# Down projection of a hybrid decoder block: weight sums on VectorE, half-row weight loads, the residual added late

## The chip, the cores and the metric

The kernel runs on one core of one Trainium2 chip. The metric is the device time of one execution in microseconds (us), as the median of repeated runs. Engines are named as the profile names them: PE (TensorE matmul) with PEld (its weight loads), DVE (VectorE), ACT (ScalarE), POOL (GpSimd) and SP (SyncE, which here only issues DMAs).

## The reference

A decoder block on 1024 tokens of width 1024, all in float32: a token mixer (forgetting attention beside HGRN2), a cross-attention over 256 memory rows, and a gated ConvFFN. Each is wrapped in `LN(ALPHA * x + f(x))`. Only the last part matters here:

```
u = x @ w_up                      # 1024 x 1024 by 1024 x 5632
u = causal_conv3(u) + conv_b      # per channel
a, g = split(u)
ff = (silu(g) * a) @ w_down       # 1024 x 2816 by 2816 x 1024
x = layer_norm(ALPHA * x + ff, ln3_g, ln3_b)
```

## The kernel before

float32 products are made from two fp32r parts. `split` (L181 on) makes them: ACT casts a tile to its high part (L183), and DVE or POOL subtracts that from the tile to get the low part (L185). Each product then takes three matmuls: high by high, high by low, low by high.

**Up stage** (L1080 and around). 22 blocks `f` of 128 hidden channels. `begin(f)` and `end(f)` run seven Strassen-Winograd products per block, the convolution and the gate follow on ACT and DVE, and the hidden tile `za` (128 channels x 1024 tokens) is written to DRAM as `hid_dram[f]` (L1125). POOL splits the weights of this stage (L1047) and forms some of their sums (L1024).

**Down stage** (L1162 on). The product with `w_down` is again Strassen-Winograd: halves over tokens, over the 22 hidden blocks (11 and 11, `HC`) and over output columns. `plan` lists seven **passes** q = 0..6. Each names a factor A of hidden tiles (A11, S3, S2, A22, S1, A12, S4), a factor B of weight rows (B11, T3, T2, T4, T1, B21, B22), and which group of four PSUM banks it accumulates in. A pass has 11 **steps** i, and a step is four token tiles by three matmuls, 12 matmuls 128x128 by 128x512 (L1239). Pass 6 runs four steps, and then the last seven (`DROWS`) for one token tile after the other, so that the closing LayerNorm can follow row by row.

For each step `load_step(q, i)` prepares two operands, called `dop`:

- `rows_of` loads hidden tiles into `raw`, a ring of three buffers. For S3, S2, S1 and S4 DVE adds or subtracts two of them (L1204). S3 and S2 are also stored to DRAM (L1206), since later passes build on them.
- `factor` fetches weight rows with `row(half, i)` (L1167 to L1172, one load of 512 KB into a 4 KB-a-partition slot `wr`) and forms T3, T2, T4, T1 in place, on POOL (L1179, L1181, L1183, L1185). It asks for both halves in every pass but the first. The slots of half 0 are given up after T1 (pass 4); from pass 5 on `factor` calls `row(0, i)` again, which loads those 11 rows a second time.
- both are split, with the subtraction on DVE.

Steps are prepared up to seven ahead (`DAHEAD`) if at least four of the 47 slots are free. Slots are handed out first in, first out.

The output rows `ys` (eight tiles of 128 x 1024) are loaded from `x2_dram` before passes 0 and 1 (L1246). After a pass, DVE moves the four banks out: the first part of a half row as `y = ALPHA*y + ps` (`scaled`, L1262), later ones as `y = y + ps` (`added`, L1263, L1285). After pass 4 rows 4 to 7 are finished and get their LayerNorm; after pass 6 rows 0 to 3. `layer_norm` takes statistics and a scale on DVE (L782, L787), a power on POOL (L785), a scale on ACT (L793) and adds the bias on POOL (L794). The store follows on SP, and the slot is given back.

**What sets the order.** The program is written in the order above, but a scheduler in the build moves instructions: it places each on its engine when its own estimate says that the inputs are ready. On the chip each engine then runs its list strictly in order, so an instruction that waits holds up all behind it on its engine. This holds for SP too, whose list is made of DMA issues.

Of the kernel before, what the change touches and what calls it, by code (L numbers as in the profile page):

```python
# [15 lines left out]
P = 128  # L16
# [86 lines left out]
def hybrid_block(ctx: ExitStack, tc: tile.TileContext, x, mem, w_in, b_fox_f, lb_logits, norm_g, w_out,  # L103
# [180 lines left out]
    def hs(half):  # L284
        return slice(half * 512, (half + 1) * 512)
# [819 lines left out]
    def end(f):  # L1105
        ya, yg, pa = live.pop(f)
        pc, pd = bank("t"), bank("t")
        product(f, "S3", "T3", pc, True)
        nc.scalar.copy(yg[:, hs(1)], pc)  # L1109
        product(f, "S1", "T1", pd, True)  # L1110
        nc.vector.tensor_tensor(yg[:, hs(1)], yg[:, hs(1)], pd, ALU.add)
        product(f, "S2", "T2", pa, False)
        u = small.tile([P, 512], F32, tag="vT", name="u", bufs=1)
        nc.scalar.copy(u, pa)
        nc.vector.tensor_tensor(yg[:, hs(1)], yg[:, hs(1)], u, ALU.add)
        product(f, "A22", "T4", pc, False)
# [48 lines left out]
    wrow, loaded = {}, {}  # L1165

    def row(half, i):  # L1167
        if (half, i) not in wrow:
            wrow[half, i] = get([P, 2, 512], name="wr")
            r = (half * HC + i) * P  # L1170
            nc.sync.dma_start(wrow[half, i].rearrange("p n c -> p (n c)"), w_down[r:r + P, :])
        return wrow[half, i]  # L1172

    def factor(name, i):

        lo, hi = row(0, i), row(1, i) if name != "B11" else None
        tt = nc.gpsimd.tensor_tensor
        if name == "T3":
            tt(lo[:, 1], hi[:, 1], lo[:, 1], ALU.subtract)  # L1179
        if name == "T2":  # L1180
            tt(lo[:, 1], lo[:, 1], lo[:, 0], ALU.add)  # L1181
        if name == "T4":
            tt(lo[:, 0], hi[:, 0], lo[:, 1], ALU.subtract)  # L1183
        if name == "T1":
            tt(lo[:, 1], hi[:, 1], lo[:, 1], ALU.subtract)  # L1185
        if name in ("B21", "B22"):
            return hi[:, int(name == "B22")]
        return lo[:, int(name not in ("B11", "T4"))]

    def rows_of(name, i):  # L1190

        h0, h1, s3, s2 = hid_dram[i], hid_dram[HC + i], sum_dram[0][i], sum_dram[1][i]
        a11, a12, a22 = h0[:, hs(0)], h1[:, hs(0)], h1[:, hs(1)]
        if name in ("A11", "A12", "A22"):
            raw = rawp.tile([P, 512], F32, tag="raw", name="raw")
            nc.sync.dma_start(raw, {"A11": a11, "A12": a12, "A22": a22}[name])
            return raw
        raw = rawp.tile([P, 2, 512], F32, tag="raw", name="raw")
        if name == "S3":
            nc.sync.dma_start(raw.rearrange("p j s -> p (j s)"), h0)  # L1200
        else:
            for j, src in enumerate({"S2": (a22, s3), "S1": (s2, a11), "S4": (a12, s2)}[name]):
                nc.sync.dma_start(raw[:, j], src)
        nc.vector.tensor_tensor(raw[:, 0], raw[:, 0], raw[:, 1], ALU.add if name == "S1" else ALU.subtract)  # L1204
        if name in ("S3", "S2"):
            nc.sync.dma_start(s3 if name == "S3" else s2, raw[:, 0])  # L1206
# [24 lines left out]
    for q, (a, b, g, first) in enumerate(plan):  # L1231
        if first:
            groups[g] = [bank(tag) for tag in (("S", "S", "S", "t"), ("t", "t", "pj", "pj"))[g]]

        def part(t, i, lo=0, hi=512):
            x, w = loaded[q, i]
            ss = slice(t * P, (t + 1) * P)
            for n, (xp, wp) in enumerate(((0, 0), (0, 1), (1, 0))):
                nc.tensor.matmul(groups[g][t][:, lo:hi], x[:, xp, ss], w[:, wp, lo:hi],  # L1239
                                 start=first and i == 0 and n == 0, stop=i == HC - 1 and n == 2,  # L1240
                                 skip_group_check=not first)

        if q < 2:
            for t in range(4 * q, 4 * q + 4):
                ys[t] = get([P, D], name="y")
                nc.sync.dma_start(ys[t], x2_dram[t * P:(t + 1) * P, :])  # L1246
        if q == 4:
            gb = load_gb(ln3_g, ln3_b)
        last = q == len(plan) - 1
        inner = HC - DROWS if last else HC  # L1250
        for i in range(inner):
            fill(q * HC + i + DAHEAD)
            for t in range(4):
                part(t, i)
# [65 lines left out]
```

## Time and profile before

| | us |
|---|---|
| median of 3 runs | 1637.95 (1633.11 to 1639.56) |
| the profiled execution: its own time | 1632.78 |
| its span (first to last instruction) | 1630.9 |
| DVE busy in the span | 1093.8 (67%) |
| POOL busy in the span | 702.9 (43%) |
| down stage, first to last matmul | 1359.87 to 1621.01 |

Times in the trace count from the span's start. In a list of groups, a line is: source line, engine, operation, tiles out<-in, shape, count, then busy time, mean duration in ns, and idle time of that engine just before, with what ended it. In a timeline, a line is start, length, engine, line, operation, and in brackets the idle time before it with its releaser. In a table of windows, each engine has its busy time and its number of instructions; the last three columns are the granted TensorE clock (1 is the full 2.4 GHz, 0.5 is 1.2 GHz), the share of time that the DMA engines were busy, and GB/s.

### The profile page before, as it was taken

What the parts mean: (1) busy time and instruction counts of PE and PEld (TensorE: products, weight loads), DVE (VectorE), ACT (ScalarE), POOL (GpSimd) and SP (SyncE); (2) the same over time, 40 slices, a digit from 0 to 9 for tenths busy, and PEclk for the clock granted to TensorE, in tenths of its full rate; (3) what the DMA queues carried; (4) which work ended last, traced back from release to release, by engine and by line L of the source; (5) the groups of instructions that cost most, each with busy time, mean ns of one, the idle gap of its engine ahead of it and who ended that gap; (6) DMA issues with size and microseconds to landing.
All of it is one profiled execution on the core that took longest, in us unless ns stands there. A gap on an engine that the chain in (4) does not pass through costs nothing.

```text
span 1630.9 us, 21374 instructions
## 1 busy us (share of the span) xinstructions
PE 1552.6 (95%) x7949; PEld 1305.6 (80%) x7949; DVE 1093.8 (67%) x1698; ACT 734.9 (45%) x1301; POOL 702.9 (43%) x540
## 2 busy tenths in 40 slices
PE   8999998999998999999999999999999998789977
PEld 6788887888887988888978877888888887668856
DVE  3856967567667756623567568777666679787777
ACT  4726554256657742133442154454544445234341
POOL 5302122233436731112003658787677774850053
PEclk9999999999999999999999999999999999899989
DMA  5301112222132673202472212232222247765763
GB/s 182 78 1 27 53 52 61 60 75 78 46 111 66 181 238 110 103 27 65 138 239 78 91 39 78 95 100 78 78 78 91 79 162 255 259 221 185 259 219 109
DMA packets 164455, 185.31 MB, mean 114 GB/s; under 512 B 7584, under 2 KB 122344, under 8 KB 164352
## 3 DMA queue, kind: packets, MB, share of 16 engines
q1 hardware_dynamic: 160864, 172.26, 33.5%
q10 hardware_dynamic: 3168, 11.54, 1.9%
q8 instruction: 62, 1.02, 0.3%
q14 instruction: 41, 0.34, 0.1%
q0 software_dynamic: 320, 0.16, 0.1%
HBM read 141.42 MB, written 38.31 MB: 110 GB/s over the span
## 4 chain that ended last, share of the span: by engine, by line
PE 64%; DVE 14%; DMA 10%; POOL 4%; ACT 4%; issue 3%; SPq 0%; DVEq 0%; POOLq 0%; ACTq 0%
PE ps_pj L174 19%; PE ps_S L174 17%; PE ps_t L1080 11%; PE ps_S L1080 6%; PE ps_t L174 4%; DVE dop L185 3%; PE ps_pj L1080 3%; DMA raw<-hid 3%; DMA raw<-sumS 2%; DVE raw L1204 1%; DMA raw<-in_w_out_dram 1%; PE ps_t L650 1%; POOL y L794 1%; POOL wop L1047 1%; PE ps_t L213 1%
## 5 line engine op out<-in xcount | busy, mean ns | idle before, releaser
L174 PE MATMUL ps_pj<-xT,wh 128*128 128x512 f32 x976 | 313.0, 396 | 0.9 <-DVE KL L593 0.9
L185 POOL TENSOR_TENSOR wl<-raw,wh 128x1024 fp32r<-128x1024 f32 x48 | 120.6, 2512 | 223.3 <-ACT wh L183 208.5
L174 PEld LDWEIGHTS ps_pj<-xT,wh 128*128 128x128 f32 x976 | 180.0, 188 | 35.2 <-DVE KL L593 1.4
L1080 PE MATMUL ps_t<-T,wop 128*128 128x512 f32 x792 | 191.9, 393 | 2.8 <-ACT yg L1109 2.1
L174 PE MATMUL ps_pj<-xT,wl 128*128 128x512 f32 x488 | 192.6, 395 | 0.0
L1080 PEld LDWEIGHTS ps_t<-T,wop 128*128 128x128 f32 x792 | 149.2, 189 | 35.2 <-ACT yg L1109 2.5
L1047 POOL TENSOR_TENSOR wop<-raw,wop 128x512 fp32r<-128x512 f32 x66 | 110.7, 1689 | 89.3 <-ACT wop L1046 89.2
L1047 POOL TENSOR_TENSOR wop<-sw,wop 128x512 fp32r<-128x512 f32 x88 | 135.3, 1560 | 21.8 <-ACT wop L1046 21.8
L784 POOL TENSOR_SCALAR mv<-mv 128x1 f32<-128x1 f32 x24 | 24.3, 1016 | 256.0 <-DVE mv L783 256.0
L1239 PE MATMUL ps_S<-dop,dop 128*128 128x512 f32 x396 | 104.5, 406 | 13.2 <-DVE dop L185 12.6
L1239 PE MATMUL ps_t<-dop,dop 128*128 128x512 f32 (+1 forms) x351 | 94.9, 392 | 19.7 <-ACT dop L183 13.1
L174 PEld LDWEIGHTS ps_pj<-xT,wl 128*128 128x128 f32 x488 | 91.8, 188 | 17.6
L1239 PEld LDWEIGHTS ps_S<-dop,dop 128*128 128x128 f32 x396 | 76.2, 195 | 34.3 <-DVE dop L185 17.0
L174 PE MATMUL ps_S<-wh,mh 128*128 128x512 f32 x256 | 100.1, 391 | 0.6 <-ACT mh L183 0.6
L174 PE MATMUL ps_S<-wh,ml 128*128 128x512 f32 x256 | 100.2, 392 | 0.0
L174 PE MATMUL ps_S<-wl,mh 128*128 128x512 f32 x256 | 99.9, 390 | 0.0
L183 ACT CAST dop<-raw 128x512 fp32r<-128x512 f32 x77 | 47.5, 620 | 105.6 <-DVE raw L1204 73.1
L1239 PEld LDWEIGHTS ps_t<-dop,dop 128*128 128x128 f32 x351 | 65.0, 195 | 36.4 <-ACT dop L183 15.2
L183 ACT CAST wh<-raw 128x1024 fp32r<-128x1024 f32 x64 | 67.2, 1050 | 59.8 <-issue 23.3
L1046 ACT CAST wop<-sw 128x512 fp32r<-128x512 f32 x88 | 54.6, 622 | 86.2 <-POOL sw L1024 57.9
L185 DVE TENSOR_TENSOR dop<-raw,dop 128x512 fp32r<-128x512 f32 x77 | 65.4, 855 | 17.4 <-ACT dop L183 16.5
L185 DVE TENSOR_TENSOR dop<-wr,dop 128x512 fp32r<-128x512 f32 x77 | 67.2, 886 | 10.9 <-ACT dop L183 10.8
(299 smaller groups left out, 3608.9 us busy)
## 6 DMA issues: line engine op xcount, KB each, us to landing
raw<-in_ffn_w_up_dram SPq DMA_DIRECT2D x44, 512.0 KB, 3.9
raw<-hid SPq DMA_DIRECT2D x66, 256.0 KB, 3.6
wr<-in_ffn_w_down_dram SPq DMA_DIRECT2D x33, 512.0 KB, 5.6
raw<-in_w_in_dram SPq DMA_DIRECT2D x24, 512.0 KB, 4.0
hid<-z SPq DMA_DIRECT2D x22, 512.0 KB, 2.6
raw<-sumS SPq DMA_DIRECT2D x33, 256.0 KB, 4.2
raw<-in_xa_wkv_dram SPq DMA_DIRECT2D x16, 512.0 KB, 4.5
x_dram<-y ACTq DMA_DIRECT2D x16, 512.0 KB, 2.6
```

The costliest lines, as they stand in the source:

```text
L174: nc.tensor.matmul(o, l, r, start=start, stop=stop)
L183: nc.scalar.copy(h, src)
L185: eng.tensor_tensor(l, src, h.bitcast(F32), ALU.subtract)
L213: nc.tensor.transpose(ps[:, k * P:(k + 1) * P], nat[:, kk * P:(kk + 1) * P], ident)
L650: nc.tensor.transpose(tp[:, b * P:(b + 1) * P], pr[1 - b % 2][:, c * P:(c + 1) * P], ident)
L784: nc.gpsimd.tensor_scalar(mv[:, 2:3], mv[:, 1:2], LN_EPS, None, ALU.add)
L794: nc.gpsimd.tensor_tensor(yp, yp, b[:, lo:hi], ALU.add)
L1046: nc.scalar.copy(w[:, 0], src)
L1047: nc.gpsimd.tensor_tensor(w[:, 1], src, w[:, 0].bitcast(F32), ALU.subtract)
L1080: nc.tensor.matmul(ps, w[:, part, ws], r, start=first and k == 0 and i == 0, stop=k == 3 and i == 2, skip_group_check=not first)
L1204: nc.vector.tensor_tensor(raw[:, 0], raw[:, 0], raw[:, 1], ALU.add if name == "S1" else ALU.subtract)
L1239: nc.tensor.matmul(groups[g][t][:, lo:hi], x[:, xp, ss], w[:, wp, lo:hi], start=first and i == 0 and n == 0, stop=i == HC - 1 and n == 2, ...
```

## The change

Six edits, all but the first in the down stage:

- **S3 made in the up stage.** For the first 11 blocks `f`, DVE subtracts the two token halves of `za` right after the gate, and SP stores the result to `sum_dram`. Pass 1 then loads 256 KB a step in place of 512 KB, with no DVE operation and no store.
- **Sums of weights on DVE.** T3, T2, T4 and T1 move from POOL to DVE, 44 instructions of 128x512.
- **Weight rows in halves.** `row(half, n, i)` loads 256 KB, one column half, when it is first asked for. Passes 5 and 6 no longer ask for half 0, so its 11 reloads are gone.
- **First parts by ACT.** The 16 `scaled` moves become plain copies on ACT (`taken`).
- **Residual late.** `x2` rows are loaded in passes 4 and 5 (steps 4 to 7) into a slot, and DVE adds them with `y = ALPHA*x + y` (L1261, 128x1024, eight times).
- **Output rows keep their slots** to the end, and `ln3`'s gains are loaded at step 3 of pass 4.

```diff
         nc.sync.dma_start(hid_dram[f], za)
+        if f < HC:
+            s3 = get([P, 512], name="s3")
+            nc.vector.tensor_tensor(s3, za[:, hs(0)], za[:, hs(1)], ALU.subtract)
+            nc.sync.dma_start(sum_dram[0][f], s3)
+            put(s3)
...
-    def row(half, i):
+    def row(half, n, i):
         if (half, i) not in wrow:
             wrow[half, i] = get([P, 2, 512], name="wr")
+        t = wrow[half, i][:, n]
+        if (half, n, i) not in here:
+            here.add((half, n, i))
             r = (half * HC + i) * P
-            nc.sync.dma_start(wrow[half, i].rearrange("p n c -> p (n c)"), w_down[r:r + P, :])
-        return wrow[half, i]
+            nc.sync.dma_start(t, w_down[r:r + P, hs(n)])
+        return t
...
-        lo, hi = row(0, i), row(1, i) if name != "B11" else None
-        tt = nc.gpsimd.tensor_tensor
+        tt = nc.vector.tensor_tensor
+        if name in ("B11", "B21", "B22"):
+            return row(int(name[1]) - 1, int(name[2]) - 1, i)
+        t = row(0, int(name != "T4"), i)
         if name == "T3":
-            tt(lo[:, 1], hi[:, 1], lo[:, 1], ALU.subtract)
+            tt(t, row(1, 1, i), t, ALU.subtract)
...
-                nc.sync.dma_start(ys[t], x2_dram[t * P:(t + 1) * P, :])
...
+            if (q in (4, 5)) and 4 <= i < 8:
+                t = i - 4 if q == 5 else i
+                x = get([P, D], name="x2")
+                nc.sync.dma_start(x, x2_dram[t * P:(t + 1) * P, :])
+                nc.vector.scalar_tensor_tensor(ys[t], x, ALPHA, ys[t], ALU.mult, ALU.add)
+                put(x)
...
-            scaled = lambda y, cs: nc.vector.scalar_tensor_tensor(y[:, cs], y[:, cs], ALPHA, ps, ALU.mult, ALU.add)
+            taken = lambda y, cs: nc.scalar.copy(y[:, cs], ps)
...
-                put(y)
```

The first place is DVE's list in pass 0. In the kernel before, `dop_11902` and `dop_11924` are the weight operands of steps 6 and 7, `z_11817` is the last hidden tile of the up stage:

```order
L1123 TENSOR_TENSOR z_11817<-z_11817,z_11799 128x1024
L185 TENSOR_TENSOR dop_12090<-wr_11867,dop_12090 128x512
L185 TENSOR_TENSOR dop_11902<-wr_11897,dop_11902 128x512
L185 TENSOR_TENSOR dop_11965<-raw,dop_11965 128x512
L185 TENSOR_TENSOR dop_11987<-raw,dop_11987 128x512
L185 TENSOR_TENSOR dop_12115<-wr_11877,dop_12115 128x512
L185 TENSOR_TENSOR dop_11921<-raw,dop_11921 128x512
L185 TENSOR_TENSOR dop_11924<-wr_11919,dop_11924 128x512
```

In the changed kernel, steps 6 and 7 have the weight operands `dop_11931` and `dop_11953`; the last hidden tile stands two rows above these:

```order
L1190 TENSOR_TENSOR wr_11916<-wr_12157,wr_11916 128x512
L185 TENSOR_TENSOR dop_11931<-wr_11926,dop_11931 128x512
L1194 TENSOR_TENSOR wr_11876<-wr_12061,wr_11876 128x512
L1192 TENSOR_TENSOR wr_11886<-wr_11886 128x512
L185 TENSOR_TENSOR dop_12139<-wr_11906,dop_12139 128x512
L1192 TENSOR_TENSOR wr_11896<-wr_11896 128x512
L185 TENSOR_TENSOR dop_12016<-raw,dop_12016 128x512
L185 TENSOR_TENSOR dop_12163<-wr_11916,dop_12163 128x512
L1194 TENSOR_TENSOR wr_11886<-wr_12085,wr_11886 128x512
L185 TENSOR_TENSOR dop_11950<-raw,dop_11950 128x512
L1192 TENSOR_TENSOR wr_11906<-wr_11906 128x512
L185 TENSOR_TENSOR dop_11953<-wr_11948,dop_11953 128x512
```

The sums L1190 (T3, for pass 1), L1192 (T2, for pass 2) and L1194 (T4, for pass 3) now stand between the operands that pass 0 waits for.

The second place is SP's list around the start of pass 6. In the kernel before, rows 4 to 7 are stored (`out_dram`) after the loads of step 1, and a reload of half 0 (`wr_13324`) stands among them:

```order
L1203 DMA raw<-hid_7591 128x512
L1203 DMA raw<-sumS_1_7613 128x512
L1290 DMA out_dram<-y_12163 128x1024
L1290 DMA out_dram<-y_12165 128x1024
L1203 DMA raw<-hid_7592 128x512
L1203 DMA raw<-sumS_2_7614 128x512
L1203 DMA raw<-hid_7593 128x512
L1290 DMA out_dram<-y_12167 128x1024
L1171 DMA wr_13324<-in_ffn_w_down_dram 128x1024
L1203 DMA raw<-sumS_3_7615 128x512
L1290 DMA out_dram<-y_12169 128x1024
```

In the changed kernel:

```order
L1207 DMA raw<-sumS_4_7616 128x512
L1207 DMA raw<-hid_7595 128x512
L1207 DMA raw<-sumS_5_7617 128x512
L1300 DMA out_dram<-y_12186 128x1024
L1300 DMA out_dram<-y_12187 128x1024
L1207 DMA raw<-hid_7596 128x512
L1300 DMA out_dram<-y_12188 128x1024
L1207 DMA raw<-sumS_6_7618 128x512
L1300 DMA out_dram<-y_12189 128x1024
L1207 DMA raw<-hid_7597 128x512
```

The stores now come after the loads of step 5, and no reload is left.

## Rows read from the trace of the kernel before

**Rows 1.** Line L1239 (the down matmuls): what its engine waited for, us, times.

```profile
  DVE dop L185: 43.0, 26
  ACT dop L183: 30.0, 14
```

**Rows 2.** Windows: an up stretch, passes 0 to 4, then 5 and 6 together.

```profile
core 0: us, PE busy (x) PEld busy (x) DVE busy (x) ACT busy (x) POOL busy (x), PEclk, DMA share, GB/s
960.00:1160.00 200.00, 196.95 (x871) 161.81 (x870) 143.38 (x131) 99.31 (x143) 152.53 (x94) 0.99 0.25 79
...
1359.90:1409.50 49.60, 39.88 (x150) 31.53 (x149) 43.11 (x38) 17.85 (x28) 33.72 (x20) 0.86 0.76 273
1409.50:1448.90 39.40, 32.13 (x130) 24.48 (x128) 33.96 (x30) 11.46 (x19) 30.75 (x20) 0.96 0.64 219
1448.90:1482.90 34.00, 31.63 (x132) 24.44 (x133) 25.83 (x35) 11.89 (x21) 7.49 (x5) 1.00 0.71 235
1482.90:1513.20 30.30, 30.21 (x133) 24.70 (x132) 24.95 (x41) 14.79 (x26) 0.00 (x0) 1.00 0.50 156
1513.20:1544.10 30.90, 30.27 (x134) 24.72 (x133) 22.24 (x36) 11.38 (x20) 0.00 (x0) 1.00 0.80 266
1544.10:1621.00 76.90, 64.10 (x286) 51.63 (x284) 57.48 (x86) 27.50 (x44) 30.33 (x20) 0.91 0.51 174
```

**Rows 3.** PE's timeline at five places of the down stage.

```profile
1396.05 2.93 PE L1239 MATMUL ps_S<-dop,dop 128*128 128x512 f32 x6 [3.98 <-DVE dop L185]
...
1484.29 1.52 PE L1239 MATMUL ps_pj<-dop,dop 128*128 128x512 f32 x6
1485.65 1.52 PE L1239 MATMUL ps_t<-dop,dop 128*128 128x512 f32 x6
...
1564.47 1.52 PE L1239 MATMUL ps_pj<-dop,dop 128*128 128x512 f32 x6
1576.31 0.80 PE L1239 MATMUL ps_t<-dop,dop 128*128 128x512 f32 x1 [10.31 <-ACT dop L183]
...
1618.24 2.77 PE L1239 MATMUL ps_t<-dop,dop 128*128 128x256 f32 x21 [0.89 <-DVE y L1285]
```

**Rows 4.** L185 on DVE, ns min/median/max, in 1360:1400 and in 1490:1540.

```profile
L185 DVE TENSOR_TENSOR dop<-wr,dop x13: 676/693/1774, 1359.5 to 1395.9; 128x512 fp32r<-128x512 f32 x13
...
L185 DVE TENSOR_TENSOR dop<-wr,dop x19: 675/684/693, 1497.1 to 1532.4; 128x512 fp32r<-128x512 f32 x19
```

**Rows 5.** DVE's timeline, end of the up stage and pass 5.

```profile
1351.04 1.27 DVE L1100 SCALAR_TENSOR_TENSOR z<-yg,cw,z 128x1023 f32<-128x1023 f32 x1
...
1362.44 0.69 DVE L185 TENSOR_TENSOR dop<-wr,dop 128x512 fp32r<-128x512 f32 x1
1363.04 0.68 DVE L1117 TENSOR_TENSOR yg<-u,ps_t 128x512 f32<-128x512 f32 x1
...
1568.22 0.69 DVE L185 TENSOR_TENSOR dop<-wr,dop 128x512 fp32r<-128x512 f32 x1
```

**Rows 6.** POOL's groups in 1290:1631, and its timeline at two places.

```profile
L1179 POOL TENSOR_TENSOR wr<-wr,wr 128x512 f32<-128x512 f32 x11 | 17.2, 1568 | 17.7 <-DMA wr<-in_ffn_w_down_dram 17.7
...
1365.20 1.29 POOL L1179 TENSOR_TENSOR wr<-wr,wr 128x512 f32<-128x512 f32 x1 [15.24 <-DMA wr<-in_ffn_w_down_dram]
...
1565.68 14.61 POOL L794 TENSOR_TENSOR y<-y,b 128x1024 f32<-128x1024 f32 x4
```

**Rows 7.** DMA issues, count, KB each, median us to landing.

```profile
wr<-in_ffn_w_down_dram SPq DMA_DIRECT2D x33, 512.0 KB, 5.6
raw<-sumS SPq DMA_DIRECT2D x33, 256.0 KB, 4.2
...
sumS<-raw SPq DMA_DIRECT2D x22, 256.0 KB, 3.2
```

**Rows 8.** SP's timeline in pass 5.

```profile
1560.76 0.43 SPq L1203 DMA_DIRECT2D raw<-sumS  x1
1572.94 2.63 SPq L1290 DMA_DIRECT2D out_dram<-y  x2
```

More of the change, by code (lines that the diff above doesn't have):

```diff
@@ L1164, in hybrid_block @@
     steps = [(q, i) for q in range(len(plan)) for i in range(HC)]
-    wrow, loaded = {}, {}
-    def row(half, i):
+    wrow, here, loaded = {}, set(), {}
+    def row(half, n, i):
         if (half, i) not in wrow:
             wrow[half, i] = get([P, 2, 512], name="wr")
+        t = wrow[half, i][:, n]
+        if (half, n, i) not in here:
+            here.add((half, n, i))
             r = (half * HC + i) * P
-            nc.sync.dma_start(wrow[half, i].rearrange("p n c -> p (n c)"), w_down[r:r + P, :])
-        return wrow[half, i]
+            nc.sync.dma_start(t, w_down[r:r + P, hs(n)])
+        return t
     def factor(name, i):
-        lo, hi = row(0, i), row(1, i) if name != "B11" else None
-        tt = nc.gpsimd.tensor_tensor
+        tt = nc.vector.tensor_tensor
+        if name in ("B11", "B21", "B22"):
+            return row(int(name[1]) - 1, int(name[2]) - 1, i)
+        t = row(0, int(name != "T4"), i)
         if name == "T3":
-            tt(lo[:, 1], hi[:, 1], lo[:, 1], ALU.subtract)
+            tt(t, row(1, 1, i), t, ALU.subtract)
         if name == "T2":
-            tt(lo[:, 1], lo[:, 1], lo[:, 0], ALU.add)
+            tt(t, t, row(0, 0, i), ALU.add)
         if name == "T4":
-            tt(lo[:, 0], hi[:, 0], lo[:, 1], ALU.subtract)
+            tt(t, row(1, 0, i), row(0, 1, i), ALU.subtract)
         if name == "T1":
[L1185 to L1188, printed above, removed]
+            tt(t, row(1, 1, i), t, ALU.subtract)
+        return t
     def rows_of(name, i):
@@ L1193, in rows_of @@
         a11, a12, a22 = h0[:, hs(0)], h1[:, hs(0)], h1[:, hs(1)]
[L1194 to L1197, printed above, removed]
+        src = {"A11": (a11,), "A12": (a12,), "A22": (a22,), "S3": (s3,), "S2": (a22, s3), "S1": (s2, a11),
+               "S4": (a12, s2)}[name]
         raw = rawp.tile([P, 2, 512], F32, tag="raw", name="raw")
[L1199 to L1206, printed above, removed]
+        for j, x in enumerate(src):
+            nc.sync.dma_start(raw[:, j], x)
+        if len(src) == 2:
+            nc.vector.tensor_tensor(raw[:, 0], raw[:, 0], raw[:, 1], ALU.add if name == "S1" else ALU.subtract)
+        if name == "S2":
+            nc.sync.dma_start(s2, raw[:, 0])
         return raw[:, 0]
@@ L1245, in hybrid_block @@
                 ys[t] = get([P, D], name="y")
-                nc.sync.dma_start(ys[t], x2_dram[t * P:(t + 1) * P, :])
-        if q == 4:
-            gb = load_gb(ln3_g, ln3_b)
         last = q == len(plan) - 1
@@ L1252, in hybrid_block @@
             fill(q * HC + i + DAHEAD)
+            if q == 4 and i == 3:
+                gb = load_gb(ln3_g, ln3_b)
+            if (q in (4, 5)) and 4 <= i < 8:
[4 more added lines that the diff above has]
+                put(x)
             for t in range(4):
@@ L1261, in hybrid_block @@
             y1, y2 = ys[t], ys[4 + t] if q else None
-            scaled = lambda y, cs: nc.vector.scalar_tensor_tensor(y[:, cs], y[:, cs], ALPHA, ps, ALU.mult, ALU.add)
+            taken = lambda y, cs: nc.scalar.copy(y[:, cs], ps)
             added = lambda y, cs: nc.vector.tensor_tensor(y[:, cs], y[:, cs], ps, ALU.add)
             if q == 0:
-                scaled(y1, n1)
+                taken(y1, n1)
             elif q == 1:
-                scaled(y2, n2)
+                taken(y2, n2)
             elif q == 2:
-                scaled(y1, n2)
-                scaled(y2, n1)
+                taken(y1, n2)
+                taken(y2, n1)
                 added(y2, n2)
```

## The prediction

> **What bounds the kernel now.** I read the waits of the down matmuls first, then a table of windows by pass, then the timelines of PE, DVE, POOL and SP where the table showed a loss.
>
> The first view [rows 1] shows that the down matmuls wait for operand splits alone: 43.0 us where DVE's subtraction came last and 30.0 us where ACT's cast did (sums over weight loads and matmuls, so not a loss in us). What is behind these waits differs from place to place.
>
> The price of a matmul comes from an undisturbed stretch [rows 3]: six start every 1.36 us (1484.29, 1485.65), so one costs 0.2267 us, a step of 12 costs 2.72 and a pass 29.9. The 42 half-width ones at the end cost 2.77 / 21 = 0.13 each. In the windows [rows 2], passes 0 to 4 take 49.6, 39.4, 34.0, 30.3 and 30.9 us; pass 0 holds 12 matmuls of the up stage (2.7 us). The losses are 17.0, 9.5, 4.1, 0.4 and 1.0. Passes 5 and 6 take 76.9 against 29.9 + 111 x 0.2267 + 42 x 0.13 = 60.5, a loss of 16.4. In all 48.4 us are lost, and the up stretch ahead has PE busy for 196.95 of 200 us. So the down stage can give at most about 48 us, in three places:
>
> - Passes 0 and 1 (26.5 us): DVE is short of time. POOL is busy for 64 of these 89 us [rows 2], and while it works, a DVE subtraction with both operands in SBUF takes up to 1.77 us in place of 0.69 [rows 4]. With POOL at rest all 19 of them stay within 0.675 to 0.693.
> - Pass 2 (4.1 us): the same, weaker, and raw buffers that are held until the S2 store has landed.
> - Passes 5 and 6 (16.4 us): SP issues nothing from 1560.76 until the output store at 1572.94 [rows 8]. That store waits for POOL's four bias adds, 14.61 us from 1565.68 [rows 6]. Behind it stand the loads of pass 6 and a reload whose slot a stored row must give back. PE stops from 1565 and goes on at 1576.31 after 10.31 us of wait [rows 3].
>
> **The change, part by part.**
>
> *Weight sums on DVE.* 44 instructions leave POOL. At rest, DVE starts one of that size every 0.60 us (1362.44, 1363.04 [rows 5]), so they cost it 26.4 us. In return nothing of POOL's runs from the last up split to the LayerNorm after pass 4, so every subtraction there costs 0.60. In steady state DVE's work for a step is 2 splits, at most 1 sum of hidden tiles and 1 of weights: 4 x 0.60 = 2.4 us in passes 2 and 4, 1.8 in 1, 3 and 6, 1.2 in 0 and 5. All are under PE's 2.72. The engine is therefore fast enough once it is ahead. The question is pass 0, where it is not: DVE's new list (the change's first place) puts sums for passes 1 to 3 between the operands that PE waits for.
>
> I count that place row by row. L1117 of the last up block started at 1363.04 [rows 5], and in both lists 23 rows lie between the hidden tile of block 19 and it, so I let it start there again. From it, 38 rows stand before the split that PE needs next (the first of pass 1; the scheduler put eight matmuls of pass 1 ahead of the end of step 7). Five are 1024 wide at 1.27 us [rows 5], 33 at 0.60: 6.4 + 19.8, and 0.7 for the split itself, gives 1389.9. To this I add 3 us for sums that wait for a row half still in flight (POOL's first sum could start at 1365.20 only when its row had landed [rows 6]). So PE goes on at about 1392.9, where it went on from the same position at 1396.05 [rows 3]. The gain is 3 us, from which I take 1 for the lower clock that follows a stop (0.86 in this pass [rows 2]). Both ends: 10 us gained if no sum waits and the early sums cost no more than the count, 10 lost if each of the first ten waits 1.3 us. I take **-2**.
>
> After that, DVE's list holds 31 rows to the end of pass 1's operands, 18.6 us, while PE has 52 matmuls left in front and then nearly all of pass 1, 37 us, before it needs the last of them. DVE is then ahead, so pass 1's loss of 9.5 should go but for 0.5: **-9**. Pass 2's loop over the three raw buffers is 4.2 to land, 0.7 for the sum and 3.2 for the store [rows 7], 8.1 / 3 = 2.7 us a step, as fast as PE, and it starts with the lead from pass 1: **-3.5** of 4.1. Passes 3 and 4: **0**. The four residual adds in pass 4 (and four in pass 5) at 1.27 us fit in DVE's idle time, 30.9 - 22.2 us in pass 4 [rows 2].
>
> *Loads in halves, no reloads, S3 made early.* Bytes a step: pass 0 goes from 768 to 512 KB, pass 1 from 1280 (two loads and a store) to 768, passes 5 and 6 lose 5.6 MB. Pass 0 ran at 273 GB/s with DMA busy for 0.76 of the time [rows 2], so this relieves a resource that was not full. I count nothing for it beyond the waits removed above. Double the number of weight loads costs SP issue time only.
>
> *Output rows keep their slots; the order on SP.* The stores of rows 4 to 7 now stand after the loads of step 5 of pass 6 (the second place), and no load waits for a stored row's slot. So the 10.31 us stop goes. What is late next is DVE: from the move-out after pass 4 to the last operand of pass 6 its list has 59 rows, 8 of them 1024 wide, 4 tiny: 47 x 0.60 + 8 x 1.27 + 0.6 = 39 us, and some 8 us more while POOL's four adds run (14.61 us [rows 6]; a DVE row there cost 0.69 at 1568.22 [rows 5] and elsewhere beside POOL up to 1.77 [rows 4], so I take about half). That is 47 us. PE needs the last operand after pass 5, four steps of pass 6 and the first six of the last seven for one tile: 29.9 + 10.9 + 4.1 = 44.9. So 2 to 3 us remain lost in place of 16.4; bounds 0 and 13 (DVE a pass-4 move-out late by 10 us). I take **-13.5**.
>
> The Trainium skill, "SBUF — State Buffer", section "Who interferes with whom", says that a VectorE instruction with two SBUF inputs and a GpSimd one that reads SBUF exclude each other, and that whichever comes second waits for the whole of the first. By that rule DVE could lose all of the 14.6 us to the four adds, passes 5 and 6 would lose 9 and the forecast would be some 6 us later; or nothing, if DVE is first each time. Step and price agree with 1.77 against 0.69 [rows 4], and the row of 0.69 in the middle of POOL's adds [rows 5] shows the second outcome as well, so I stay at half.
>
> *First parts by ACT.* 16 moves leave DVE (0.60 each, 10 us); ACT has them at about 0.6 with 75% of its time free in passes 0 to 4. They stand behind six or seven prepared steps in ACT's list, 16 to 19 us of PE work, so I count **0**.
>
> *S3 in the up stage.* 11 DVE subtractions of 0.69 to 1.77 us. DVE is idle for 57 of the 200 us of that stretch and PE for 3 [rows 2]. Bounds 0 and 19.5; I take **+1**, near the row, since PE hardly waits there.
>
> **Sum.** -2 - 9 - 3.5 - 13.5 + 1 = -27. Counted the other way, PE at 1392.9 has 836 matmuls left, 190.3 us at the undisturbed price; with 1 us for the clock, 3 of loss and 1 from the up stage its last one ends at 1588, 33 us before 1621. (The difference is what pass 0 lost after 1396.05.) I take the middle, -30: the profiled execution, 1632.8 us with 1.9 of it outside its span, would go to 1603. The median of the runs is 5.2 us above the profiled execution; on the median the forecast is 1638 - 30 = **1608 us**.
>
> **Rivals.**
>
> *PE is never short again* (15%). If early sums never wait and POOL waits for DVE in the LayerNorm rather than the reverse, pass 0 gains 10 and passes 5 and 6 all 16.4: 10 + 9.5 + 4.1 + 16.4 + 1.4 = 41, so about 1596. For it: DVE's load of 1.2 to 2.4 us a step. Against: 38 rows in front of one operand.
>
> *Only part of it comes* (18%). DVE meets ACT's casts late in the new order, as it did before, and pass 0 loses 8 more; the LayerNorm still holds 10 us in passes 5 and 6. Then -30 + 8 + 7 = -15: 1623.
>
> *DVE stands where POOL stood* (slower, 6%). POOL waited 17.7 us for weight rows to land before T3 alone [rows 6]; nobody stood behind it. Now each such wait holds up every split. Halves come by separate loads, so T4 has such a wait too. If both cost DVE 17.7 us, and the 26.4 us of work adds to it, DVE loses 62 us in passes 0 and 1 and wins back some 30 us of contention (68 instructions in 77.1 us there [rows 2], against 47 at 0.69): +32, less 17 from passes 2, 5 and 6, gives 1653. It decides from about 1.3 us of wait on each of 22 first sums. Against it: all row loads now stand ahead of the hidden tiles of pass 1 in SP's list.
>
> The Trainium skill, "DMA: Bandwidth & Descriptors", section "Measured (HBM→SBUF, 128 partitions, SWDGE, issued from GpSimd)", speaks for this rival: it says to batch transfers to 1 MiB or more. By rows, 256 KB land in 4.2 us and 512 KB in 5.6 [rows 7], so two halves one behind the other would cost 2.8 us more for each of 22 rows; pass 0 ran at 273 GB/s with loads of both sizes in flight, and I keep the low chance.
>
> *No change* (6%): contention falls, but the front of pass 0 eats it all, 1630 to 1646.
>
> **Chances and range.** The forecast itself, 1600 to 1618, has 55%. Faster by over 0.5% (8 us, about what a measurement here can tell from no change) is 55 + 15 + 18 = 88%, same 6%, slower 6%. The range for 8 in 10 is 1588 to 1629: it takes in most of both faster rivals and leaves out the last two.
>
> **What would show it.** Right: L185 and the sums on DVE within 0.7 us from the end of the up stage until pass 5; POOL idle there; PE going on within pass 0 before 1394 after a stop of several us; passes 1 to 4 at 30 to 31 us; no gap over 3 us on SP in pass 5; passes 5 and 6 in 61 to 65 us. Wrong: DVE rows waiting for weight loads by more than 1 us each; passes 2 or 4 over 33 us, which would make DVE or the raw ring the bound; a PE stop of over 6 us in pass 6; or PE idle in the up stage by more than it is now.

## The result, and the profile after

The changed kernel takes 1619.15 us (median of 4 runs, 1616.52 to 1620.13) against 1638.2 us for the kernel before on the same chip: a ratio of 0.9887, 95% interval 0.9863 to 0.9911, or 19 us less. The forecast was 1608 us and the range 1588 to 1629; the forecast's own band, 1600 to 1618, just misses it. The profiled execution took 1620.13 us with a span of 1618.4 us, against 1632.78 and 1630.9.

The first table cuts the span by stage. "Up" runs from the first matmul of L1080 to the first down matmul. The passes are cut where the matmuls change between the banks ps_S and ps_pj, which agrees with [rows 2] within 1 us. Passes 0 and 1 stand together, since some matmuls of pass 1 run inside pass 0. "Undisturbed" is 0.2267 us a matmul, as in the prediction.

| | before up | up | passes 0+1 | 2 to 4 | 5+6 | after the last matmul |
|---|---|---|---|---|---|---|
| undisturbed | | | 59.8 | 89.7 | 60.5 | |
| before | 924.6 | 435.2 | 88.8 | 95.5 | 76.7 | 9.9 |
| after | 929.5 | 450.7 | 68.4 | 89.7 | 72.4 | 7.6 |
| difference | +4.9 | **+15.5** | **-20.4** | -5.8 | -4.3 | -2.3 |

The +4.9 is no work of the change. That stretch has the same instructions in every kernel of this study, and over 14 profiles it took 924.6 to 936.2 us. So stages are compared by profile, and whole kernels by medians.

Here are the windows of the kernel after, with the columns of [rows 2]: the same up stretch, then passes 0, 1 and 4, and passes 5 and 6 together. Passes 2 and 3 read like pass 4: PE 29.90 of 29.90 us, POOL 0.00.

```profile
960.00:1160.00 200.00, 191.74 (x844) 156.17 (x843) 149.97 (x132) 89.90 (x132) 142.50 (x85) 0.99 0.26 86
...
1380.20:1420.40 40.20, 36.82 (x154) 29.28 (x153) 38.19 (x59) 21.73 (x35) 0.00 (x0) 0.96 0.81 276
1420.40:1448.50 28.10, 28.10 (x126) 23.27 (x125) 24.05 (x41) 12.78 (x24) 0.00 (x0) 1.00 0.75 244
...
1508.30:1538.25 29.95, 29.95 (x133) 24.77 (x132) 25.96 (x39) 13.80 (x25) 0.00 (x0) 1.00 0.70 235
1538.25:1610.85 72.60, 65.44 (x286) 52.63 (x284) 59.62 (x78) 20.69 (x29) 29.36 (x21) 0.93 0.43 146
```

From pass 1 to pass 4 PE is busy all the time and POOL does nothing. The loss sits in the first row, in pass 0 and in the last row. In the up stretch PE ran 844 matmuls in 200 us where it ran 871 [rows 2].

What the up matmuls of L1080 waited for in the kernel after (us, times; matmuls and weight loads added):

```profile
  DVE yg L1111: 31.4, 20
```

In the kernel before the same line reads:

```profile
  DVE yg L1111: 2.8, 3
```

L1111 reads the PSUM bank into which the last product of a block then goes on adding. DVE's timeline of the kernel after shows what stands ahead of it:

```profile
1102.81 1.72 DVE L1123 TENSOR_TENSOR z<-z,z 128x1024 f32<-128x1024 f32 x1
1104.57 1.66 DVE L1128 TENSOR_TENSOR s<-z 128x512 f32<-128x512 f32 x1
1106.15 0.68 DVE L1111 TENSOR_TENSOR yg<-yg,ps_t 128x512 f32<-128x512 f32 x1
1110.66 0.69 DVE L1024 TENSOR_TENSOR sw<-sw,raw 128x512 f32<-128x512 f32 x1 [3.83 <-POOL sw L1024]
```

L1128 is S3, the new subtraction. It takes 1.66 us, L1111 follows it, and then DVE stands for POOL's weight sum. Two theories fit these four rows. By the first, S3's time ahead of L1111 is the cost. By the second, S3's extra buffer turns the free list, so that the weight sums get other buffers and come late. The lists of both kernels speak for the second. POOL's first L1024 of a block waited for PE before, which had long finished with that buffer. Now it waits for DVE, and it stands behind two splits of weight rows (L1047) instead of ahead of them. POOL's timeline, before and then after:

```profile
1064.84 2.29 POOL L1024 TENSOR_TENSOR sw<-raw 128x512 f32<-128x512 f32 x1
1069.94 4.16 POOL L1047 TENSOR_TENSOR wop<-raw,wop 128x512 fp32r<-128x512 f32 x2 [2.82 <-ACT wop L1046]
```

```profile
1101.53 4.16 POOL L1047 TENSOR_TENSOR wop<-raw,wop 128x512 fp32r<-128x512 f32 x2 [2.82 <-ACT wop L1046]
1105.64 1.72 POOL L1024 TENSOR_TENSOR sw<-raw 128x512 f32<-128x512 f32 x1
```

In the down stage these are PE's rows with a wait in pass 0 of the kernel after, and the one with the longest in pass 6:

```profile
1400.62 0.96 PE L1244 MATMUL ps_S<-dop,dop 128*128 128x512 f32 x3 [1.22 <-ACT dop L183]
1403.97 2.42 PE L1244 MATMUL ps_S<-dop,dop 128*128 128x512 f32 x6 [2.16 <-DVE dop L185]
...
1586.02 1.65 PE L1244 MATMUL ps_S<-dop,dop 128*128 128x512 f32 x3 [3.10 <-DVE dop L185]
```

The 10.31 us stop of pass 5 [rows 3] is gone, and pass 6 has stops of its own.

### The profile page after: what moved, and what is told of

It reads as the page before. It is cut to its first block, busy times and chain, and to the rows that moved or that the text cites. A ratio compares the mean times of both kernels' runs of the same rounds, so it can differ in the third digit from the quotient of the medians.

```text
span 1618.4 us, 21414 instructions
## 1 busy us (share of the span) xinstructions
PE 1552.2 (96%) x7949; PEld 1307.9 (81%) x7949; DVE 1104.0 (68%) x1734; ACT 739.8 (46%) x1317; POOL 642.8 (40%) x496
## 4 chain that ended last, share of the span: by engine, by line
PE 61%; DVE 15%; DMA 8%; POOL 6%; ACT 4%; issue 4%; SPq 1%; POOLq 0%; DVEq 0%; ACTq 0%
PE ps_pj L174 22%; PE ps_S L174 17%; PE ps_t L1080 7%; PE ps_t L174 5%; PE ps_S L1080 3%; POOL wop L1047 3%; DVE dop L185 2%; DMA raw<-hid 2%; POOL sw L1024 2%; DMA raw<-sumS 2%; DVE sw L1024 2%; PE ps_pj L1080 2%; PE ps_S L1244 1%; DVE z L1101 1%; DVE z L1100 1%
## 5 line engine op out<-in xcount | busy, mean ns | idle before, releaser
L185 POOL TENSOR_TENSOR wl<-raw,wh 128x1024 fp32r<-128x1024 f32 x48 | 118.0, 2457 | 219.7 <-ACT wh L183 206.2
L1080 PE MATMUL ps_t<-T,wop 128*128 128x512 f32 x792 | 190.2, 391 | 1.5 <-ACT yg L1109 0.9
L1080 PEld LDWEIGHTS ps_t<-T,wop 128*128 128x128 f32 x792 | 148.1, 188 | 33.5 <-ACT yg L1109 1.3
L1047 POOL TENSOR_TENSOR wop<-raw,wop 128x512 fp32r<-128x512 f32 x66 | 119.7, 1826 | 94.4 <-ACT wop L1046 94.4
L1047 POOL TENSOR_TENSOR wop<-sw,wop 128x512 fp32r<-128x512 f32 x88 | 135.6, 1562 | 28.9 <-ACT wop L1046 28.9
L174 PEld LDWEIGHTS ps_pj<-xT,wl 128*128 128x128 f32 x488 | 91.9, 188 | 17.7
L1244 PE MATMUL ps_t<-dop,dop 128*128 128x512 f32 (+1 forms) x351 | 87.1, 378 | 1.7 <-DVE y L1295 1.7
L183 ACT CAST dop<-raw 128x512 fp32r<-128x512 f32 x77 | 47.7, 622 | 85.7 <-DVE raw L1209 44.9
L1080 PE MATMUL ps_t<-B,wop 128*128 128x512 f32 x264 | 68.9, 410 | 13.6 <-DVE yg L1111 13.6
L1080 PEld LDWEIGHTS ps_t<-B,wop 128*128 128x128 f32 x264 | 50.8, 196 | 28.3 <-DVE yg L1111 17.8
```

Of the source, the lines that this page charges most:

```text
L174: nc.tensor.matmul(o, l, r, start=start, stop=stop)
L183: nc.scalar.copy(h, src)
L185: eng.tensor_tensor(l, src, h.bitcast(F32), ALU.subtract)
L1047: nc.gpsimd.tensor_tensor(w[:, 1], src, w[:, 0].bitcast(F32), ALU.subtract)
L1080: nc.tensor.matmul(ps, w[:, part, ws], r, start=first and k == 0 and i == 0, stop=k == 3 and i == 2, skip_group_check=not first)
```

## The experiments

Each kernel is compared with the kernel before on the same chip. The chip differs between e1 to e4, e5 to e8, e9 to e11 and e12, so across these groups the ratio counts and not the median. Stages are in us, cut as above.

| kernel | median | ratio, 95% interval | up | 0+1 | 2 to 4 | 5+6 |
|---|---|---|---|---|---|---|
| after | 1619.2 | 0.9887 [0.9863, 0.9911] | 450.7 | 68.4 | 89.7 | 72.4 |
| e1_s3_newest | 1612.9 | 0.9864 [0.9847, 0.9881] | 447.9 | 69.2 | 89.7 | 72.8 |
| e2_before_turn | 1667.4 | 1.0199 [1.0172, 1.0227] | 465.6 | 87.7 | 96.5 | 78.6 |
| e3_s3_down | 1623.2 | 0.9926 [0.9909, 0.9943] | 435.3 | 74.9 | 94.6 | 80.6 |
| e4_pool_sums | 1633.4 | 0.9991 [0.9968, 1.0013] | 452.0 | 76.4 | 89.7 | 77.3 |
| e5_s3_u_buffer | 1605.2 | 0.9806 [0.9776, 0.9836] | 436.8 | 69.2 | 89.7 | 71.7 |
| e6_res_early | 1604.8 | 0.9807 [0.9779, 0.9834] | 438.2 | 69.3 | 89.7 | 71.7 |
| e7_act_store | 1606.3 | 0.9823 [0.9789, 0.9858] | 436.9 | 69.5 | 89.7 | 72.8 |
| e8_ln_dve | 1599.0 | 0.9780 [0.9740, 0.9820] | 437.0 | 68.7 | 89.7 | 64.8 |
| e9_res_early_ln_dve | 1598.1 | 0.9764 [0.9735, 0.9794] | 436.5 | 69.5 | 89.7 | 63.6 |
| e10_before_no_reload | 1637.8 | 1.0006 [0.9983, 1.0030] | 435.4 | 88.3 | 95.0 | 78.5 |
| e11_before_ln_dve | 1631.6 | 0.9977 [0.9954, 0.9999] | 435.4 | 88.0 | 95.3 | 70.5 |
| e12_before_dve_sums | 1617.7 | 0.9896 [0.9864, 0.9928] | 435.2 | 70.2 | 98.3 | 74.5 |

### The up stage: S3's time, or its buffer

**e1_s3_newest** keeps the subtraction and takes its buffer so that the others stay where they were.

```diff
-            s3 = get([P, 512], name="s3")
+            s3 = slots.get_newest([P, 512], name="s3")
```

> The changed kernel, but the buffer of S3 is taken from the newest end of the free list and so given back where it was: every other tile gets the buffer that it had in the kernel before. The subtraction stays on VectorE, between L1123 and L1111. Theory A (the turn of the buffers: S3's extra get moves the weight sums of L1024 onto buffers that VectorE reads late, so POOL makes them late): the up stage, from the first L1080 matmul to the first of the down stage, goes from 450.7 us back to 435 to 440, the whole to 1604 to 1609. Theory B (the subtraction of 1.66 us itself, ahead of L1111 on VectorE): 449 to 451, the whole stays at 1619.

**e2_before_turn** does the reverse: the kernel before, with the turn and without the subtraction.

```diff
         nc.sync.dma_start(hid_dram[f], za)
+        if f < HC:
+            put(get([P, 512], name="s3"))
         put(za)
```

> The kernel before, with one buffer taken and given back without use in each of the first 11 blocks of the up stage, where the changed kernel takes S3's. No instruction is added. Theory A (turn of the buffers): the up stage goes from 435.3 us to 445 to 451, the whole to 1648 to 1654. Theory B (the subtraction itself): 435, the whole 1638.

e1 got back only 2.8 us in the up stage, outside A's range and just below B's 449. e2, which adds no instruction, lost 30.4 us in the up stage, more than A had said and nothing that B allows. So a turn of the buffers alone can cost twice what the change lost there, and yet setting it right did little. A line of the L1080 waits of e2, then a row each of POOL's timeline in e2 and in e1, explain this:

```profile
  DVE yg L1111: 48.0, 20
```

```profile
1120.51 1.29 POOL L1024 TENSOR_TENSOR sw<-raw 128x512 f32<-128x512 f32 x1 [2.84 <-DMA raw<-in_ffn_w_up_dram]
```

```profile
1104.77 1.28 POOL L1024 TENSOR_TENSOR sw<-raw 128x512 f32<-128x512 f32 x1 [1.03 <-DMA sumS<-s]
```

In e2 PE waits for the same L1111, now 48.0 us, and POOL's sum waits 2.84 us for raw weights in its new place in the list. In e1 the sum waits 1.03 us for the *store* of S3: the buffer that S3 took is the one that the next sum gets, and the store still reads it. So e1 had removed one wait and made another.

**e5_s3_u_buffer** gives S3 a buffer outside the free list, that of u.

```diff
-            s3 = get([P, 512], name="s3")
+            s3 = small.tile([P, 512], F32, tag="vT", name="s3", bufs=1)
...
-            put(s3)
```

> The changed kernel with S3 in the buffer of u (a half row outside the free list), so that S3 neither turns the buffers nor lets its store hold one of them. The subtraction stays on VectorE. Theory A, as mended by the two runs on the turn (what is left in e1_s3_newest is the store of S3, which holds the buffer that POOL's next sum wants, 1.03 us in each block): the up stage 435 to 440 us, the whole 1598 to 1605. Theory B (1.66 us more on VectorE ahead of L1111): 446 to 449, the whole 1611 to 1615.

The up stage is back at 436.8 us and the whole at 1605.2, at the edge of what theory A gave. The window of the up stretch of e5 (columns as above), and the row of S3 (ns min/median/max):

```profile
960.00:1160.00 200.00, 196.07 (x867) 161.65 (x866) 155.75 (x137) 95.91 (x138) 152.76 (x91) 0.98 0.27 90
```

```profile
L1128 DVE TENSOR_TENSOR s<-z x11: 1649/1666/1667, 986.1 to 1174.8; 128x512 f32<-128x512 f32 x11
```

S3 is still there, 11 times 1.66 us ahead of L1111, and PE runs 867 matmuls; POOL's first L1024 of a block waits for PE again. The subtraction itself costs 436.8 - 435.2 = 1.6 us; the other 13.9 of the 15.5 us came from its buffer. Theory B falls.

**e3_s3_down** asks whether S3 belongs in the up stage at all: it makes S3 in pass 1 as before.

```diff
-        if f < HC:
-            s3 = get([P, 512], name="s3")
-            ...
+        if name == "S3":
+            nc.sync.dma_start(raw.rearrange("p j s -> p (j s)"), h0)
...
+        if name in ("S3", "S2"):
+            nc.sync.dma_start(s3 if name == "S3" else s2, raw[:, 0])
```

> The changed kernel with S3 made in pass 1 of the down stage as in the kernel before (one 512 KB load, subtraction on VectorE, store), all else as changed. Both A and B: the up stage back to 435 us. Pass 1 then carries on VectorE per step two splits, a weight sum and this subtraction, 4 x 0.69 = 2.76 us against 2.72 us of matmuls: 0 to 4 us lost there; the whole 1604 to 1609. If the 15 us in the up stage were not S3's doing: 1619 or more.

The up stage came back to 435.3 as both theories said, but the down stage lost 19.6 us (6.5, 4.9 and 8.2), where 0 to 4 was expected. PE's longest wait of e3, in pass 6:

```profile
1573.76 3.78 PE L1242 MATMUL ps_S<-dop,dop 128*128 128x512 f32 x8 [4.14 <-DVE dop L185]
```

So the place of S3 is right and only its buffer was wrong. In pass 6 the stretch of DVE in which POOL's biases fall is the same as in the kernel after, row for row, but it comes 9.0 us later against PE: its add of 3.43 us starts 26.9 us after the first `ps_pj` matmul of pass 5 (1559.43 and 1532.51) and in the kernel after 17.9 us (1557.54 and 1539.61). What made DVE late by then was not taken apart.

### Passes 0 to 2: the engine of the weight sums

**e4_pool_sums** is the changed kernel with the sums on POOL, and **e12_before_dve_sums** the kernel before with the sums on DVE. Each is one word; e12 has it the other way round.

```diff
-        tt = nc.vector.tensor_tensor
+        tt = nc.gpsimd.tensor_tensor
```

> The changed kernel with the weight sums of the down stage on POOL again. If the gain of passes 0 to 2 comes from the sums' engine: passes 0 to 2 lose again most of the 30.6 us that they lost before (17.0, 9.5, 4.1; now 5.8 in all), 12 to 25 us more than the changed kernel, 1631 to 1644. If it comes from the half rows or the evacuation by ACT: within 3 us of 1619.

> The kernel before with the weight sums of the down stage on VectorE; no other edit. If the sums' engine is what pass 0 lost by (theory E): pass 0 goes from 48.7 us to 40 to 43, pass 1, where S3 is still made, from 40.1 to 33 to 37, pass 2 stays within 1 us of 34.4, the whole 1622 to 1630. Rival (half rows and the evacuation by ACT brought it, and POOL's sums cost only in the changed kernel's order): pass 0 stays at 47 to 49, the whole within 3 us of 1635.

e4 lost 8.0 us in passes 0 and 1, nothing in passes 2 to 4, and 4.9 in passes 5 and 6. In passes 0 to 2 that is less than the 12 to 25 expected; the whole stands level with the kernel before and came into its range by the other stages. e12 won 18.6 us in passes 0 and 1 with nothing else changed, more than expected, and gave 2.8 back in passes 2 to 4, where pass 2 was to stay within 1 us. Its ratio, 0.9896, is that of the whole change. What its down matmuls waited for, the lines that answer to [rows 1]:

```profile
  ACT dop L183: 24.9, 9
  DVE dop L185: 18.8, 13
```

DVE's splits fell from 43.0 to 18.8 us.

The two runs do not add up to one price. With the sums on POOL, the rest of the change still makes passes 0 and 1 12.4 us shorter than before (e4, 76.4 against 88.8); the sums' engine alone makes them 18.6 shorter (e12); both together 20.4. So the sums' engine is enough for most of the gain there, but part of it comes without it. In passes 2 to 4 it is the other way: e4 has no loss with the sums on POOL, and e12, which still makes S3 in pass 1, keeps one. What half rows and ACT's copies did by themselves was not separated.

The rest of the change took part of this away in the up stage, won part by S3's move, and came out even.

### Passes 5 and 6: the reload, the residual adds, the stores, or POOL

All of e6 to e9 stand on e5. **e6_res_early** moves four residual adds from pass 5 to pass 3, **e7_act_store** moves the stores of pass 4's rows to ACT's queue, and **e8_ln_dve** ends the LayerNorm of these rows on DVE.

```diff
-            if (q in (4, 5)) and 4 <= i < 8:
-                t = i - 4 if q == 5 else i
+            if (q in (3, 4)) and 4 <= i < 8:
+                t = i - 4 if q == 3 else i
```

> e5_s3_u_buffer, and the residual rows 0 to 3 are loaded and added in pass 3 instead of pass 5. Theory C (pass 6 is late since VectorE is full from 1550 to 1580 us; the four adds of 1.3 to 3.4 us are part of that): passes 5 and 6 together go from 72.4 us to 63 to 68, pass 3 stays at 29.9. Theory D (the stores of the finished rows stand on SP ahead of the loads of the raw rows): 71 to 73.

```diff
-                           done=lambda lo, hi: nc.sync.dma_start(out[ss, lo:hi], y[:, lo:hi]))
+                           done=lambda lo, hi: (nc.sync if last else nc.scalar).dma_start(out[ss, lo:hi], y[:, lo:hi]))
```

> e5_s3_u_buffer, and the finished rows of pass 4 are stored by ACT's queue instead of SP's. Theory D: passes 5 and 6 together 62 to 68 us. Theory C: 71 to 73.

```diff
-  LNP if last and t == 3 else ((0, D, "pool"),)
+  LNP if last and t == 3 else ((0, D, "pool" if last else "dve"),)
```

> e5_s3_u_buffer, and the LayerNorm of the rows of pass 4 ends on VectorE (scale and bias in one instruction of some 1.3 us a row) instead of ACT and POOL. Theory C1 (VectorE's instructions are long there, 3.4 us for 1.3, since POOL adds the biases beside them): passes 5 and 6 together 64 to 69 us. Theory C2 (it is VectorE's own work that is too much): 73 to 78. Theory D: 71 to 73.

The adds alone change nothing (71.7), so theory C in that form falls. Without the stores on SP it is 72.8, so D falls. With the biases on DVE it is 64.8: C1. (By the whole, e8 and e5 cannot be told apart, since their intervals overlap; the 6.9 us stand on the stage.) POOL's and DVE's timelines of the kernel after, beside each other:

```profile
1556.76 3.13 POOL L794 TENSOR_TENSOR y<-y,b 128x1024 f32<-128x1024 f32 x1
```

```profile
1556.39 1.24 DVE L787 SCALAR_TENSOR_TENSOR y<-y,mv,g 128x1024 f32<-128x1024 f32 x1
1557.54 3.43 DVE L1261 SCALAR_TENSOR_TENSOR y<-x,y 128x1024 f32<-128x1024 f32 x1
1560.90 3.49 DVE L185 TENSOR_TENSOR dop<-wr,dop 128x512 fp32r<-128x512 f32 x2
...
1565.51 1.22 DVE L1261 SCALAR_TENSOR_TENSOR y<-x,y 128x1024 f32<-128x1024 f32 x1
1567.24 3.42 DVE L787 SCALAR_TENSOR_TENSOR y<-y,mv,g 128x1024 f32<-128x1024 f32 x1
```

The same add of L1261 takes 3.43 us beside POOL's bias and 1.22 without it. Each of the four biases lengthens one stretch of DVE by 2.1 to 2.2 us, 8.7 us in all, and DVE has no time to spare there. Windows of the kernel after and of e8, columns as above:

```profile
1560.00:1570.00 10.00, 10.00 (x46) 8.27 (x45) 10.00 (x7) 3.44 (x5) 7.48 (x4) 1.00 0.27 106
...
1580.00:1590.00 10.00, 5.41 (x15) 3.00 (x13) 8.70 (x16) 2.01 (x4) 0.00 (x0) 0.77 0.54 158
1590.00:1600.00 10.00, 9.14 (x31) 6.98 (x30) 5.03 (x8) 1.77 (x2) 3.80 (x3) 0.71 0.00 0
```

```profile
1560.00:1570.00 10.00, 10.00 (x45) 8.28 (x45) 10.00 (x14) 1.52 (x3) 0.00 (x0) 1.00 0.59 211
```

DVE reads 10.00 of 10 us in both, but does 7 instructions beside POOL and 14 without. Busy time alone would have hidden this. The lower rows show the rest of the price: after the stops of pass 6 the granted clock is 0.77 and 0.71, part of the time at the lower level (1.2 GHz), and PE is 9.14 us busy with 31 matmuls where 46 fit into 10 us before.

**e10_before_no_reload** and **e11_before_ln_dve** take the same two suspects out of the kernel before.

```diff
-        lo, hi = row(0, i), row(1, i) if name != "B11" else None
+        lo = row(0, i) if name not in ("B21", "B22") else None
+        hi = row(1, i) if name != "B11" else None
```

> The kernel before without the 11 reloads of weight rows in passes 5 and 6, which nothing reads; no other edit. As the prediction has it (SP stands at the reloads, which wait for a buffer): passes 5 and 6 together go from 75.9 us to 62 to 66. Theory C1 (the biases that POOL adds beside VectorE): 72 to 76.

(e11 has the same edit as e8.)

> The kernel before with the LayerNorm of the rows of pass 4 ended on VectorE instead of ACT and POOL; no other edit, the reloads stay. Theory C1: passes 5 and 6 together from 75.9 us to 66 to 71. As the prediction has it (the reloads that stand on SP are the limit): 74 to 77.

Without the reloads passes 5 and 6 take 78.5 us instead of 76.7 (the expectations say 75.9, 0.8 too little): nothing won, and more than either theory gave. With the LayerNorm on DVE and the reloads kept they take 70.5. SP's timeline of e10, then of e11, at the place of [rows 8], and a row of PE's of e10:

```profile
1576.04 0.43 SPq L1204 DMA_DIRECT2D raw<-sumS  x1
1585.37 3.68 SPq L1291 DMA_DIRECT2D out_dram<-y  x2
```

```profile
1570.00 0.43 SPq L1203 DMA_DIRECT2D raw<-sumS  x1
1574.57 3.92 SPq L1290 DMA_DIRECT2D out_dram<-y  x2
```

```profile
1596.62 3.78 PE L1240 MATMUL ps_S<-dop,dop 128*128 128x512 f32 x8 [3.84 <-DVE dop L185]
```

In e10 SP still stands 9 us at the store, which waits for POOL, and PE's stop moves from pass 5 to pass 6. In e11 the gap is 4.1 us. Of e11's 6.2 us the whole shows about 3.7 (0.9977); after its last matmul it has 13.6 us, 3.6 more than before.

The kernel before shows the same pair of engines the other way round. POOL's first bias there:

```profile
1565.68 7.23 POOL L794 TENSOR_TENSOR y<-y,b 128x1024 f32<-128x1024 f32 x1
```

It takes 7.23 us, the next three 2.33 to 2.81. All DVE rows beside it keep their price, among them the 0.69 of [rows 5]. So there POOL waited for DVE, and SP's store waited for POOL: 1565.68 + 7.23 = 1572.91, and the store goes out at 1572.94 [rows 8]. In e10 the first bias takes 3.09 us and DVE is the one that waits (5.66 us for two splits from 1586.35). So e10 shows that the stop does not need the reloads, but not what they cost alone, since the waiting changed sides as well. Why one engine comes first in one kernel and the other in the next was not found.

**e9_res_early_ln_dve** joins e6 and e8.

> e8_ln_dve (S3 in the buffer of u, LayerNorm of pass 4 on VectorE) with the residual rows 0 to 3 added in pass 3 as in e6_res_early. VectorE is still full from 1550 to 1570 us in e8_ln_dve. Theory C: without the four adds passes 5 and 6 together go from 64.8 us to 61 to 63, the whole to 1594 to 1599. Rival (as in e6_res_early, the adds hide): 64 to 66, the whole as e8_ln_dve, 1599.

63.6 us lies between the two expectations, and the whole, 1598.1, cannot be told from e8's 1599.0. PE no longer stops in pass 6 until the last tile: its windows of 10 us stay at 1.00 of clock and 10.00 us busy to 1580. The last of them:

```profile
1570.00:1580.00 10.00, 10.00 (x48) 8.32 (x47) 6.47 (x11) 1.77 (x2) 2.45 (x4) 1.00 0.00 0
```

It beats both kernels: 37 us less than before, 0.9764 [0.9735, 0.9794].

## Why the prediction was right or wrong

The direction and the range were right, for reasons of which half were wrong. That the total fell into the range is partly luck, since large misses of both signs met in it.

- **Weight sums on DVE** (-2 in pass 0, -9 in pass 1): the mechanism was right for most of it (e12), the size too small, -20.4 in both together, about half of it in each pass. The count of rows held: the split that it names started 27.0 us behind L1117 (1383.45 to 1410.44), of which 1.1 were a wait for a weight row, where the count gave 26.2. The 3 us for sums that wait for row halves were 1.3. What failed is, first, that PE did not stand behind that split: its first matmuls of pass 1 ran before the split began, and those behind them did not wait.

```profile
1409.50 1.07 PE L1244 MATMUL ps_pj<-dop,dop 128*128 128x512 f32 x4
```

  Second, I priced pass 0 by one stop. The kernel before had two more:

```profile
1375.75 2.70 PE L1239 MATMUL ps_S<-dop,dop 128*128 128x512 f32 x8 [1.89 <-DVE dop L185]
1387.65 2.93 PE L1239 MATMUL ps_S<-dop,dop 128*128 128x512 f32 x6 [3.86 <-DVE dop L185]
```

  With the 3.98 of [rows 3] that is 9.7 us. All three end with a split of DVE, and DVE's rows beside POOL's sums are long there (up to 1.77 us). After the change two stops of 1.22 and 2.16 are left. DVE's splits of weight rows from 1385 on (ns min/median/max) stay where the prediction had them, against up to 1774 [rows 4]:

```profile
L185 DVE TENSOR_TENSOR dop<-wr,dop x58: 674/686/695, 1385.9 to 1535.9; 128x512 fp32r<-128x512 f32 x58
```

- **Pass 2** (-3.5) and **passes 3 and 4** (0): -4.5 and -1.3 measured. The size of pass 2 was near, its reason was not: it is free of loss with the sums on POOL (e4) and loses with S3 made in pass 1 (e3, e12), so it is S3's move and not a lead of DVE by the sums.
- **S3 in the up stage** (+1): +15.5, the largest miss. The reason given, that DVE and PE have time there, was right for the subtraction, which costs 1.6 us (e5). It left out the buffer. The bounds of 0 to 19.5 held it, and the last of the signs that would make the prediction wrong named it. It could have been read blind: in POOL's list the first sum of each block changes from a wait for PE to a wait for DVE.
- **Output rows keep their slots** (-13.5): -4.3. The stop on SP was real [rows 8] and went as forecast, but it was the store's wait for POOL's first bias add alone, and not for the slot that a reload wanted: without the reloads nothing was won (e10), without the biases on POOL 6.2 us (e11). What failed is the 2 to 3 us that were to remain; 72.4 - 60.5 = 11.9 did. The count of DVE's 59 rows was near, 49.6 us from the first move-out to the end of the last split where it gave 47, and "about half" of POOL's 14.61 us, 8 us, came as 8.7. But the list began late:

```profile
1540.00 0.69 DVE L1209 TENSOR_TENSOR raw<-raw 128x512 f32<-128x512 f32 x1 [3.42 <-DMA raw<-sumS]
...
1542.41 0.68 DVE L1273 TENSOR_TENSOR y<-y,ps_S 128x512 f32<-128x512 f32 x1
...
1591.33 0.69 DVE L185 TENSOR_TENSOR dop<-raw,dop 128x512 fp32r<-128x512 f32 x1 [0.68 <-ACT dop L183]
```

  Pass 4 ended at 1538.25; the first move-out started 4.2 us later, behind a row that had waited 3.42 us for a load. So the last operand came 53.8 us after pass 4, where PE wanted it after 44.9, and was 8.9 us late. The other 3 us came behind it, and the term had nothing for them: 45 matmuls took 12.52 us, in part at the lower clock (0.71), where 10.2 are undisturbed, and PE waited 1.66 us once more for a move-out.
- **The Trainium skill**, "SBUF — State Buffer", section "Who interferes with whom": by its rule the prediction had passes 5 and 6 lose 9 us in place of 2 to 3. They lost 11.9, so the 9 was nearer, but by luck: it has DVE lose all of the 14.6 us, and DVE lost 8.7. The trace agrees with the rule on who waits, both ways: DVE behind POOL's four biases in the kernel after, POOL behind DVE in the first bias of the kernel before (7.23 us), where the row of 0.69 stands [rows 5].
- **First parts by ACT** (0): no sign of a cost in passes 1 to 4, but no run tried it alone.
- **The rivals**: of the second, at 1623, "the LayerNorm still holds 10 us in passes 5 and 6" is what came; pass 0 did better than it said. DVE did not stand where POOL stood: the first sums waited 1.3 us in all for weight rows, not 17.7.

By terms: -2 - 9 - 3.5 - 13.5 + 1 = -27 was forecast, and -20.4 - 5.8 - 4.3 + 15.5 = -15.0 came, with 2.3 more behind the last matmul. Two errors nearly met by luck, 9.4 us too little in passes 0 and 1 and 9.2 too much in passes 5 and 6, and the up stage made the rest.

Open: what makes DVE late for pass 6 when S3 is made in pass 1 (e3), how the 20.4 us of passes 0 and 1 divide among the edits that overlap there, which engine comes first when POOL and DVE meet, and which of the shifted waits makes up e2's 30 us.

## What to carry to other kernels

One more tile from a shared free list changes the buffer of every tile behind it, so compare, instruction by instruction, whom each waits for in the two lists, and give a newcomer a buffer of its own. Price an instruction on VectorE by what GpSimd does beside it, and count instructions, not busy time, to see it. Before a stop is put down to what stands first in a queue, take away that cause alone: the next one behind it may be as late.

## What the runs showed of the hardware

In the up stage POOL is busy for 142.50 of 200 us. Beside it, DVE's subtraction with both inputs in SBUF takes 1.63 to 1.78 us every time (L1128), and the operation of the same size with one input in PSUM never more than 0.683 (L1111):

```profile
L1128 DVE TENSOR_TENSOR s<-z x11: 1632/1664/1775, 986.0 to 1186.8; 128x512 f32<-128x512 f32 x11
...
L1111 DVE TENSOR_TENSOR yg<-yg,ps_t x22: 674/676/683, 957.2 to 1377.9; 128x512 f32<-128x512 f32 x22
```

The Trainium skill, "SBUF — State Buffer", section "Who interferes with whom", says that a VectorE instruction with at most one SBUF input does not contend with GpSimd. The 22 rows of L1111 agree.

The wait goes both ways. In the kernel after, DVE's add of 1.22 us took 3.43 beside a bias of POOL; in the kernel before, POOL's bias of 2.33 us took 7.23 beside DVE rows that kept their price.
